# GpSimd in place of ScalarE issues one load of a multiply-and-GELU kernel

## The chip, the cores and the metric

The kernel runs on one core of a Trainium2 chip. A core has TensorE, VectorE, ScalarE, GpSimd and SyncE, which run their own instruction streams and meet through semaphores, and 16 DMA engines that move data between the device memory and the on-chip memory. In the profile the engines are called PE, DVE, ACT, POOL and SP; a name with a q behind it (SPq, POOLq) is the engine's instruction queue, where DMA issues, drains and semaphore operations are listed.

The metric is the device time of one execution in microseconds, taken as the median of several runs. The trace comes from one profiled execution, and its span runs from the first to the last instruction of the program; a little time lies around it.

## The reference

Two matrices of 1024 x 4096 in float32 are multiplied element by element, and the tanh form of GELU is taken of the product:

```python
z = x * y
return (0.5 * z * (1 + np.tanh(np.sqrt(2 / np.pi) * (z + 0.044715 * z ** 3)))).astype(np.float32)
```

Each matrix has 16.78 MB. Two are read and one is written, 50.33 MB in all.

## The kernel before

Each matrix is taken as one flat array and cut into three pieces (PIECES, line 14). A piece is laid over the 128 partitions of the on-chip memory, so that each partition gets one contiguous row of it: piece 0 has rows of 1,280 numbers (5 KB, 0.66 MB in all), piece 1 rows of 16,384 (64 KB, 8.39 MB) and piece 2 rows of 15,104 (59 KB, 7.73 MB). All of x lies on the chip at once in `xs`; y goes through a smaller buffer `ys`, whose places are used a second time (Y_LOADS, line 16, gives the place of each y piece; Y_FREE, line 18, the number of products that must be done before a place may be loaded again).

Each load or store of a piece is one DMA instruction with a semaphore of its own, which reaches 16 when all has landed. The loads and stores go out in this order:

- SyncE issues the load of x's piece 0 as its first instruction, and ScalarE that of x's piece 1 as its own first instruction. The function `_hoist` (lines 25 to 37) takes a DMA instruction out of the body and puts it into the program's first block, ahead of the drains and barriers that the launch code places there.
- SyncE then waits for x's piece 0 (line 81), and issues y's piece 1 and x's piece 2 one behind the other (lines 82 and 83).
- SyncE waits until three products are done and issues y's piece 2 into the place that they leave free; after the fourth product it issues y's piece 0 (lines 84 to 87).
- When y's piece 2 has landed and the results of piece 1 are done, SyncE stores piece 1, then piece 2, then piece 0 (lines 112 to 116). Lines 117 to 122 wait for the stores and clear the semaphores.

VectorE multiplies `xs` by `ys` in place, in 13 steps (STEPS, line 20): four of 4,096 columns over piece 1, seven of 2,048 and one of 768 over piece 2, one of 1,280 over piece 0. ScalarE follows step by step with the GELU, in place again (lines 99 to 110).

Around the body stands code of the launch. Line 137, the making of the program object, gives GpSimd four fills of constants and gives all engines a drain and a barrier: GpSimd drains its own queue, collects a semaphore from the other engines, and releases them. Line 59 (`tc.compile()`) adds two more such barriers. The body of every engine, SyncE's wait at line 81 included, comes behind these three; the two hoisted loads come ahead of them. In the program's first block GpSimd's order is one bookkeeping instruction (INC_SWDGE_SEM), the four fills, the drain, the barrier.

Of the kernel before, what the change touches and what calls it, by code (L numbers as in the profile page):

```python
# [1 line left out]

# [4 lines left out]


F32 = mybir.dt.float32
GELU = mybir.ActivationFunctionType.Gelu_apprx_tanh  # L10

PIECES = [(0, 1280), (1280, 17664), (17664, 32768)]

Y_LOADS = [(1280, 17664, 4056), (17664, 32768, 0), (0, 1280, 15104)]

Y_FREE = [0, 3, 4]

STEPS = [[4096] * 4, [2048] * 7 + [768], [1280]]  # L20
STORES = [(1280, 17664), (17664, 32768), (0, 1280)]
Y_BUF = 20440


def _hoist(nc, issued):

    here = nc.cur_bb.bb.instructions
    first = nc.main_func.blocks[0].instructions
    for ins in issued:
        del here[next(k for k, i in enumerate(here) if i is ins or i.name == ins.name)]  # L30
    engine = issued[0].engine
    at = next(
        k
        for k, i in enumerate(first)
        if i.engine == engine and type(i).__name__ == "InstDrain"
    )
    first[at:at] = issued


@with_exitstack  # L40
def kernel(
    ctx: ExitStack,
    tc: tile.TileContext,
    x: bass.AP,
    y: bass.AP,
    out: bass.AP,
):
    nc = tc.nc
    P = nc.NUM_PARTITIONS

    def columns(t, a, b):

        flat = t.flatten_outer_dims().rearrange("r c -> (r c)")
        pa, pb = next(q for q in PIECES if q[0] <= a and b <= q[1])
        return flat[P * pa : P * pb].rearrange("(p c) -> p c", p=P)[:, a - pa : b - pa]


    tc.close()
    tc.compile()

    xs = nc.alloc_sbuf_tensor("xs", [P, PIECES[-1][1]], F32).ap()
    ys = nc.alloc_sbuf_tensor("ys", [P, Y_BUF], F32).ap()
    sem_x = [nc.alloc_semaphore(f"sem_x{i}") for i in range(len(PIECES))]
    sem_y = [nc.alloc_semaphore(f"sem_y{i}") for i in range(len(Y_LOADS))]
    sem_mul = nc.alloc_semaphore("sem_mul")
    sem_act = nc.alloc_semaphore("sem_act")
    sem_o = [nc.alloc_semaphore(f"sem_o{i}") for i in range(len(STORES))]

    def load_x(i, engine=nc.sync):
        a, b = PIECES[i]  # L70
        return engine.dma_start(out=xs[:, a:b], in_=columns(x, a, b)).then_inc(sem_x[i], 16)

    def load_y(i):
        a, b, r = Y_LOADS[i]
        return nc.sync.dma_start(
            out=ys[:, r : r + b - a], in_=columns(y, a, b)
        ).then_inc(sem_y[i], 16)

    _hoist(nc, [load_x(0).ins])
    _hoist(nc, [load_x(1, nc.scalar).ins])  # L80
    nc.sync.wait_ge(sem_x[0], 16)
    load_y(0)
    load_x(2)
    for i in range(1, len(Y_LOADS)):
        if Y_FREE[i]:
            nc.sync.wait_ge(sem_mul, Y_FREE[i])
        load_y(i)

    nc.scalar.wait_ge(sem_x[0], 16)
    n = 0  # L90
    done = {}
    for i, (a, b, r) in enumerate(Y_LOADS):
        for j, (xa, xb) in enumerate(PIECES):
            if xa <= a < xb:
                nc.vector.wait_ge(sem_x[j], 16)
        nc.vector.wait_ge(sem_y[i], 16)  # L96
        c = a
        for w in STEPS[i]:
            nc.vector.tensor_mul(  # L99
                out=xs[:, c : c + w],  # L100
                in0=xs[:, c : c + w],
                in1=ys[:, r + c - a : r + c - a + w],
            ).then_inc(sem_mul, 1)
            n += 1
            done[c + w] = n
            nc.scalar.wait_ge(sem_mul, n)
            nc.scalar.activation(  # L107
                out=xs[:, c : c + w], in_=xs[:, c : c + w], func=GELU
            ).then_inc(sem_act, 1)
            c += w  # L110

    for i, (a, b) in enumerate(STORES):
        if i == 0:
            nc.sync.wait_ge(sem_y[-2], 16)
        nc.sync.wait_ge(sem_act, done[b])
        nc.sync.dma_start(out=columns(out, a, b), in_=xs[:, a:b]).then_inc(sem_o[i], 16)
    for i in range(len(STORES) - 1):
        nc.sync.wait_ge(sem_o[i], 16)
    nums = sorted(s.num for s in [*sem_x, *sem_y, *sem_o[:-1], sem_mul, sem_act])
    assert nums == list(range(nums[0], nums[-1] + 1))  # L120
    nc.sync.sem_clear(range(nums[0], nums[-1] + 1))
    nc.sync.wait_ge(sem_o[-1], 16).then_inc(sem_o[-1], -16)


# [1 line left out]
_INS = ['x', 'y']  # L126
_OUTS = [((1024, 4096), 'float32')]


# [23 lines left out]
```

## Time and profile before

| | |
|---|---|
| median of 3 runs | 119.83 us (119.7 to 119.85) |
| span of the profiled execution | 118.5 us, so 1.3 us lie around it |
| VectorE busy | 35.2 us, 13 instructions |
| ScalarE busy | 30.9 us, 14 instructions, one of them a table load of 1.28 us |
| GpSimd busy | 0.2 us, 4 instructions |
| bytes moved | 50.33 MB, 425 GB/s over the span |

Issue to landing of each load, from the list of DMA issues: x's piece 0 in 13.6 us (issued at 0.00), x's piece 1 in 30.4 us (issued by ScalarE at 0.12), y's piece 1 in 29.0 us (issued at 13.57), x's piece 2 in 46.5 us (issued at 13.96), y's piece 2 in 22.5 us (issued at 55.79). The three stores land 20.4 to 20.9 us after their issue.

How to read it: a page has the busy time of each engine, the span in 40 equal slices with the busy share in tenths and the rate of the DMA engines, the chain of work that ended last, and the groups of instructions with what ended the idle time before them. Queue instructions (drains, semaphores, DMA issues) are not counted as busy; they are found by asking for a line of the program. Of such a group the answer gives the count, the shortest, median and longest duration in ns, and the start of the first and last in us.

### The profile page before, as it was taken

How to read it: one execution, taken by the hardware profiler on the slowest of the kernel's cores; microseconds unless marked ns; L12 is line 12 of the kernel's file. 1: busy time of each engine (PE TensorE's matmuls, PEld its weight loads, DVE VectorE, ACT ScalarE, POOL GpSimd, SP SyncE). 2: the span in 40 equal slices, each digit the busy share in tenths (PEclk: the TensorE clock that was granted, in tenths of full speed). 3: DMA queues.
4: the chain of work that ended last, by engine and by line, in shares of the span. 5: the costliest groups of instructions: out<-in, count | busy, mean ns of one | idle time of the engine just before them, and what ended most of it. 6: DMA issues, size and time to landing. Idle time of an engine off the chain costs nothing.

```text
span 118.5 us, 83 instructions
## 1 busy us (share of the span) xinstructions
DVE 35.2 (30%) x13; ACT 30.9 (26%) x14; POOL 0.2 (0%) x4
## 2 busy tenths in 40 slices
DVE  0000000000000069999920000059999940000000
ACT  0000000000000000999975000006998990000000
POOL 0000000000000000000000000000000000000000
DMA  9888899889988897798797797798899887977975
GB/s 492 382 382 382 354 597 464 354 354 465 597 354 354 354 632 347 326 632 347 326 632 347 326 632 347 326 575 354 354 531 531 354 354 326 653 326 326 653 326 221
DMA packets 1296, 50.33 MB, mean 425 GB/s; under 512 B 144, under 2 KB 144, under 8 KB 528
## 3 DMA queue, kind: packets, MB, share of 16 engines
q1 hardware_dynamic: 1152, 41.94, 82.3%
q10 hardware_dynamic: 144, 8.39, 16.5%
HBM read 33.55 MB, written 16.78 MB: 425 GB/s over the span
## 4 chain that ended last, share of the span: by engine, by line
DMA 55%; DVE 24%; ACT 3%; issue 1%; DVEq 0%
DMA ys<-in_y_dram 43%; DVE xs L99 24%; DMA xs<-in_x_dram 11%; ACT xs L107 3%; DVEq L96 0%
## 5 line engine op out<-in xcount | busy, mean ns | idle before, releaser
L99 DVE TENSOR_TENSOR xs<-xs,ys 128x2048 f32<-128x2048 f32 (+3 forms) x13 | 35.2, 2778 | 60.9 <-DMA ys<-in_y_dram 60.9
L107 ACT ACTIVATE xs<-xs 128x2048 f32<-128x2048 f32 (+3 forms) x13 | 29.6, 2300 | 19.6 <-DVE xs L99 19.6
L107 ACT ACT_TABLE_LOAD x1 | 1.3, 1283 | 47.2 <-DVE xs L99 47.2
L137 POOL MEMSET const-uint8-127<- 128x1 uint8 x1 | 0.1, 102 | 0.0
L137 POOL MEMSET const-bfloat16-1.0<- 128x1 bf16 x1 | 0.1, 101 | 0.0
L137 POOL MEMSET const-float32-0.0<- 128x1 f32 x1 | 0.1, 98 | 0.2 <-issue 0.2
L137 POOL MEMSET const-float32-1.0<- 128x1 f32 x1 | 0.1, 98 | 0.0
## 6 DMA issues: line engine op xcount, KB each, us to landing
xs<-in_x_dram SPq DMA_DIRECT2D x1, 7552.0 KB, 46.5
ys<-in_y_dram SPq DMA_DIRECT2D x1, 7552.0 KB, 22.5
out_dram<-xs SPq DMA_DIRECT2D x1, 7552.0 KB, 20.4
xs<-in_x_dram SPq DMA_DIRECT2D x1, 640.0 KB, 13.6
ys<-in_y_dram SPq DMA_DIRECT2D x1, 640.0 KB, 19.7
out_dram<-xs SPq DMA_DIRECT2D x1, 640.0 KB, 20.8
xs<-in_x_dram ACTq DMA_DIRECT2D x1, 30.4
ys<-in_y_dram SPq DMA_DIRECT2D x1, 29.0
```

The lines of the kernel that those rows point to most:

```text
L99: nc.vector.tensor_mul(out=xs[:, c : c + w], in0=xs[:, c : c + w], in1=ys[:, r + c - a : r + c - a + w],).then_inc(sem_mul, 1)
L107: nc.scalar.activation(out=xs[:, c : c + w], in_=xs[:, c : c + w], func=GELU).then_inc(sem_act, 1)
L137: nc = _bacc.Bacc("TRN2", target_bir_lowering=False, num_devices=1)
```

## The change

The load of x's piece 1 is issued by GpSimd instead of ScalarE. The hoisting function now looks for the engine's first drain or fill, whichever comes first: on GpSimd that is the first constant fill, so that the DMA stands behind INC_SWDGE_SEM and ahead of the four fills, the drain and the barriers. SyncE and ScalarE have no fills in that block, so nothing moves for the load of x's piece 0. The bytes, rows, places and semaphores stay as they are.

```diff
@@ -32,7 +32,7 @@
     at = next(
         k
         for k, i in enumerate(first)
-        if i.engine == engine and type(i).__name__ == "InstDrain"
+        if i.engine == engine and type(i).__name__ in ("InstDrain", "InstMemset")
     )
     first[at:at] = issued
 
@@ -77,7 +77,7 @@
     _hoist(nc, [load_x(0).ins])
-    _hoist(nc, [load_x(1, nc.scalar).ins])
+    _hoist(nc, [load_x(1, nc.gpsimd).ins])
     nc.sync.wait_ge(sem_x[0], 16)
     load_y(0)
     load_x(2)
```

## The prediction

> **What bounds the kernel now.** I read the slices first, then windows, the chain, the first microseconds instruction by instruction, and what SyncE's queue waits for. In slices and windows the DMA engines are full from the second microsecond to the last:
>
> ```profile
> DMA  9888899889988897798797797798899887977975
> GB/s 492 382 382 382 354 597 464 354 354 465 597 354 354 354 632 347 326 632 347 326 632 347 326 632 347 326 575 354 354 531 531 354 354 326 653 326 326 653 326 221
> ```
> ```profile
> 0.00:1.00 1.00, 0.00 (x0) 0.00 (x0) 0.20 (x4) 1.00 0.00 0
> 1.00:42.60 41.60, 0.00 (x0) 0.00 (x0) 0.00 (x0) 1.00 1.03 442
> ```
>
> The last two columns of a window are DMA share and GB/s. Nothing moves for 1.0 us, SyncE's first load starts, and then 442 GB/s go by until y's 64 KB rows (y0) have landed; 50.33 MB over the span are 425. A transfer is booked where it starts, so a share can read a little over 1. By the trace's records of single transfers the first starts at 1.01 and the last ends at 118.1, with 116.3 us of packets on each engine between: at most 0.8 us is idle. So bytes are the bound, and a change costs what it adds of empty DMA time, whichever engine computes.
>
> Which transfers must be kept supplied is in the chain (start, length, what) and in SyncE's waits:
>
> ```profile
> 0.00 13.56 DMA xs<-in_x_dram
> 13.56 0.02 issue
> 13.57 28.99 DMA ys<-in_y_dram
> 42.56 0.03 issue
> ```
> ```profile
> SPq L75 <- DVE xs L99: 45.4, 2, 41.4
> ...
> SPq L75 <- DMA xs<-in_x_dram: 12.1, 1, 12.1
> ```
>
> SyncE loads x's small piece (0.66 MB, called x0 here), waits for it (12.1 us), issues y0 at 13.57 and x's last piece (x2) at 13.96. Only ScalarE's load of x's 64 KB rows (x1, 8.39 MB) bridges the engines from about 2.3 to 17.4 us, the first transfer of y0. x0 lands so late because its rows alternate on each engine with x1's, 2.42 us a row: x0's first five rows are through when x1 starts at 2.2 to 2.6 us, and the other three and the completion mark each wait behind one row of x1. x1 is through near 27.7. There are 14 us between the issue of y0 and the end of x1, and that slack is what keeps the engines full.
>
> The beginning, by instruction and then by line:
>
> ```profile
> 0.12 0.36 ACTq L71 DMA_DIRECT2D xs<-in_x_dram  x1
> 0.23 0.10 POOL L137 MEMSET const-float32-0.0<- 128x1 f32 x1 [0.23 <-issue]
> ...
> 0.33 0.10 POOL L137 MEMSET const-uint8-127<- 128x1 uint8 x1
> ```
> ```profile
> L137 POOLq INC_SWDGE_SEM  x1: 27/27/27, 0.1 to 0.1; - x1
> ...
> L137 POOLq DRAIN  x1: 181/181/181, 0.3 to 0.3; - x1
> ...
> L137 ACTq DRAIN  x1: 145/145/145, 0.5 to 0.5; - x1
> L137 SPq EVENT_SEMAPHORE  x1: 17/17/17, 0.8 to 0.8; - x1
> ```
> ```profile
> L59 POOLq DRAIN  x2: 34/38/41, 0.9 to 1.2; - x2
> ...
> L59 SPq EVENT_SEMAPHORE  x2: 17/17/17, 1.1 to 1.5; - x2
> ```
>
> Line 137 ends with a barrier of all engines, and line 59 holds two more. GpSimd is the hub: it drains, collects the others, releases them. SyncE is out of the third barrier at 1.5, and only then can it reach its wait for x0 and the issue of y0. So y0 stands behind three drains of GpSimd's queue.
>
> **The change, part by part.** *Removed:* one issue on ScalarE, 0.36 us at 0.12. ScalarE's next work is a table load at 47.17 that waits for VectorE: worth nothing. Its drain (0.5) may come 0.36 earlier, but SyncE idles 12.1 us behind the barrier: nothing.
>
> *Added:* the same issue on GpSimd, at about 0.16, behind the 27 ns instruction and ahead of fills, DRAIN and barriers. Two prices are not in the trace.
>
> First, when x1's first row starts. Rows near it: SyncE's issue at 0.00 moves at 1.01, so 1.0 after issue; ScalarE's, at 0.12 behind SyncE's, moves at 2.2, so 2.1 after. By these GpSimd's rows start at 1.2 to 2.3. x0 alone, eight rows per engine at a mean of 0.24 us, fills the engines until 1.01 + 1.9 = 2.9. I take 2.3, within that cover, so zero; each microsecond after 2.9 costs one until y0 fills the hole. The ends are 0 and, for a start two microseconds worse than the worst row, 1.4. The Trainium skill ("DMA: Bandwidth & Descriptors", Latency and other measured facts) gives a first byte about 0.6 us after an issue from sync or scalar and about 1 us from GpSimd; our row of 1.0 is already longer than that 0.6, so the page's difference of 0.4 on that row would give an estimated start near 1.6, also under cover.
>
> Second, what stands behind the issue on GpSimd's queue: four fills (about 0.2 us), the DRAIN, the three barriers, and through them SyncE's y0 and x2 and all compute. The DRAIN's rows bound its price from both sides. ScalarE's DRAIN took 145 ns while 8.39 MB of ScalarE's own load were in flight until 30 us: a drain need not wait for a transfer. That is the low end, 0. But GpSimd's DRAIN, starting at 0.3 for 181 ns, ended at 0.48, about 0.05 after the last fill (0.33 + 0.10): it does wait for what GpSimd issued. And GpSimd alone has an instruction in this preamble that keeps count of DMA semaphores (INC_SWDGE_SEM): its DMA issues are work that the engine's own queue tracks, where ScalarE's are handed off. I take it that the DRAIN holds until x1 has landed; that is the high end, worked out now.
>
> x0 and x1 are 9.04 MB, at 425 GB/s 21.3 us from 1.01: the engines would turn to the next transfer at 22.3. For y0, 17.43 MB had gone by at its landing, 41.0 us from 1.01 or 42.0, and it was seen at 42.56; so a landing is seen some 0.5 us after the mean engine is through: x1 at 22.8. The DRAIN ends 0.05 later. From its end to SyncE's last release is now 0.48 to 1.49, 1.0 us: 23.85. SyncE's wait for x0 is long over, it issues y0 at once, and the first byte follows 1.0 us later: 24.85. The engines stand empty for 24.85 - 22.3 = 2.55 us. Off that comes about 0.2: where x1 and y0 now alternate, 12 to 27 us, an engine's records show gaps of 0.02 to 0.1 at the changes of queue, and one queue at a time mostly shows none. Net 2.35 us.
>
> Downstream all shifts alike. In both orders y0 is through when x0, x1 and y0 have gone by, x2 follows, y's second load is released by VectorE's third product (55.79) with x2 running to 60; compute, loads and stores keep their distances. No cover is lost there and none is gained.
>
> The sum: the profiled execution has a span of 118.5, and the median of the runs is 119.83, 1.3 us more, which lies around the span. 118.5 + 2.35 = 120.85 of span, 122.2 with what lies around it. Bounds for this case: a quicker way (landing seen 0.4 late, barriers at their spacing of 0.33 each, first byte after 0.85 as with the first store) adds 1.7, thus 121.5; a start of x1 a microsecond past its cover and slower barriers add 3.8, thus 123.6.
>
> **The rivals.** *The DRAIN lets go, and nothing changes.* For: ScalarE's 145 ns. Against: the 181 ns and the counting instruction above. Then a start of x1 anywhere between 1.5 and 2.9 only moves x0's landing between some 3 and 20 us; y0 is issued before x1 is through (22 at the earliest), and the engines never run dry: 119.8. The Trainium skill says as much of a change of issuer ("DMA: Bandwidth & Descriptors", Issuing engines are not separate DMA queues): the transfers run on the same 16 engines and interleave whoever starts them, so only issue time is saved. The trace bears that out for two queues from 2.3 to 27.7 us, and for the barrier no row decides.
>
> *The DRAIN lets go, but GpSimd's rows come late.* From 2.9 until x1 starts the engines are empty. x0 then lands near 3.2, y0 is issued at 3.6 and moves by 4.6, so the hole is 1.7 at most: 120.2 to 121.5. For: no row shows a GpSimd issue, and it is the engine's first work. Against: 2.1 us is the worst row. If GpSimd also cut the rows smaller, x1 would fall behind y0 and land late; no row speaks for it.
>
> *The DRAIN lets go, and GpSimd's rows come too early.* If x1 starts before 1.5, x0's rows alternate with all eight of x1, and x0 lands only when x1 is through: the hole is landing, issue and first byte, 0.4 + 1.0 + 0.2 of spread: 121.4. For: SyncE's 1.0 us. Against: GpSimd would have to be as quick as that.
>
> *Faster.* One mechanism: with the alternation gone, or x1's first row sooner, some of the 0.8 us of idle DMA time between first and last transfer goes. It decides only if the DRAIN lets go and over 0.24 is won: 119.2 to 119.5. Against: the first byte at 1.01 is SyncE's and untouched, and most of the gaps lie behind 27 us.
>
> **How the numbers follow.** DRAIN holds: 0.70, 122.2, its own range 121.5 to 123.6. No change: 0.17. Late: 0.07. Too early: 0.03. Faster: 0.03. A measurement of this kernel tells 0.2% (0.24 us) from no change; so slower 0.70 + 0.07 + 0.03 = 0.80, same 0.17, faster 0.03. The case's own range holds some 0.63, and with late and too early about 0.72; to leave out no more than 0.2 it must reach the unchanged time: 119.6 to 123.6.
>
> **What would show it.** In the profile after: GpSimd's DRAIN of line 137 lasting some 22 us, SyncE's releases at lines 137 and 59 near 23 to 24 us, y0 issued near 24 with a landing 18 to 19 us later, x1 landing 22 to 23 us after its issue, a DMA-free stretch of over 2 us before 25 us, and VectorE starting near 45 instead of 42.66. Wrong it would be if that DRAIN stays under a microsecond; then x0's landing and the issue of y0 tell which rival it is. If the DRAIN holds and the loss is small, then a landing is seen sooner, or the barriers pass quicker, than their rows say.

## The result, and the profile after

The changed kernel takes 124.61 us (median of 4 runs, 124.13 to 124.8), the kernel before 119.8 us beside it. The ratio is 1.0398, with a 95% interval of 1.0383 to 1.0413: slower by 4.8 us. The forecast was 122.2 us, in a range of 119.6 to 123.6: the measured time lies 1.0 us above its upper end. The sign was right, its mechanism was right, and its size was half of the true one. A run more than 1.5% above the fastest of its kernel counts as slow and stands in no ratio: below, one of six in the changed kernel's second series, and three of four, the profiled one among them, with a quarter of x1 on GpSimd.

The profiled execution of the changed kernel has a span of 123.7 us and a time of 124.53. The first instructions, then parts of lines 137 and 59 (count, shortest/median/longest in ns, start of the first and last in us); three dots stand for lines left out:

```profile
0.00 0.38 SPq L71 DMA_DIRECT2D xs<-in_x_dram  x1
0.72 0.65 POOL L71 DMA_DIRECT2D xs<-in_x_dram  x1 [0.72 <-issue]
1.37 0.12 POOL L137 MEMSET const-float32-0.0<- 128x1 f32 x1
...
25.91 0.33 SPq L75 DMA_DIRECT2D ys<-in_y_dram  x1
```
```profile
L137 POOLq EVENT_SEMAPHORE  x2: 17/17/17, 25.1 to 25.1; - x2
...
L137 ACTq DRAIN  x1: 8/8/8, 0.1 to 0.1; - x1
...
L137 PEldq DRAIN  x1: 8/8/8, 0.3 to 0.3; - x1
L137 SPq DRAIN  x1: 131/131/131, 0.4 to 0.4; - x1
L137 POOLq DRAIN  x1: 24212/24212/24212, 0.8 to 0.8; - x1
...
L137 SPq EVENT_SEMAPHORE  x1: 17/17/17, 25.2 to 25.2; - x1
```
```profile
L59 SPq EVENT_SEMAPHORE  x2: 17/17/17, 25.5 to 25.8; - x2
```

GpSimd's drain took 0.18 us before; now it takes 24.2 us, from 0.80 to 25.01. Every other engine has drained by 0.6 us. The list of issues gives the landing of GpSimd's load (last number, us after its issue at 0.72, so at 24.9):

```profile
xs<-in_x_dram POOLq DMA_DIRECT2D x1, 24.2
```

GpSimd releases them at 25.1, two more barriers pass, and SyncE issues y's 64 KB rows (y0) at 25.91, where it was 13.57. SyncE's waits and the chain say the same:

```profile
SPq L137 <- PEq L137: 24.7, 1, 24.7
```
```profile
25.85 0.06 issue
25.91 21.83 DMA ys<-in_y_dram
```

The profile puts this wait down to PE's queue, but PE had drained at 0.3: the wait is the barrier, and the only drain of it that ends near 25 us is GpSimd's.

Windows, with the last two columns DMA share and GB/s, first of the changed kernel, then of the kernel before:

```profile
1.00:23.20 22.20, 0.00 (x0) 0.00 (x0) 0.59 (x5) 1.00 0.99 407
23.20:26.60 3.40, 0.00 (x0) 0.00 (x0) 0.00 (x0) 1.00 0.00 0
26.60:47.70 21.10, 0.00 (x0) 0.00 (x0) 0.00 (x0) 1.00 1.05 443
```
```profile
23.20:26.60 3.40, 0.00 (x0) 0.00 (x0) 0.00 (x0) 1.00 0.71 308
```

In 3.4 us no transfer starts at all. From y0's landing on (47.74, before 42.56) the chain runs 5.2 us later, and its distances behind it have not changed.

The records of single transfers give the sum for a mean DMA engine (starts and ends are means over the 16 engines). The whole shift of 5.2 us of span is made before y0 has landed:

| Part | Before | After | Adds |
|---|---|---|---|
| x0's last row ends, x1's first starts | no hole | 2.99, 3.30 | 0.3 |
| rows of x1, mean of 8 per engine | 2.44 us | 2.51 us | 0.55 |
| rows of y0, mean of 8 per engine | 2.42 us | 2.50 us | 0.65 |
| rows of x0, mean of 8 per engine | 0.24 us | 0.23 us | -0.1 |
| x1's last row ends, y0's first starts | no hole | 23.36, 27.06 | 3.7 |

x0 is x's small piece and x1 its 64 KB rows, as in the prediction. The hole of 3.7 us has four pieces: 1.24 from the mean end of x1 to its last row on any engine (24.60), 0.41 until the drain ends (25.01), 0.90 through three barriers to SyncE's issue (25.91), and 1.15 to the mean first row of y0 (27.06).

### The profile page after: what moved, and what is told of

It is laid out like the page before. It is cut to its first block, busy times and chain, and to the rows that moved or that the text cites. A ratio compares the mean times of both kernels' runs of the same rounds, so it can differ in the third digit from the quotient of the medians.

```text
span 123.7 us, 83 instructions
## 1 busy us (share of the span) xinstructions
DVE 35.2 (28%) x13; ACT 30.9 (25%) x14; POOL 0.9 (1%) x5
## 4 chain that ended last, share of the span: by engine, by line
DMA 36%; DVE 23%; ACT 3%; issue 1%; DVEq 0%
DMA ys<-in_y_dram 36%; DVE xs L99 23%; ACT xs L107 3%; DVEq L96 0%
## 5 line engine op out<-in xcount | busy, mean ns | idle before, releaser
L71 POOL DMA_DIRECT2D xs<-in_x_dram x1 | 0.7, 652 | 0.7 <-issue 0.7
## 6 DMA issues: line engine op xcount, KB each, us to landing
ys<-in_y_dram SPq DMA_DIRECT2D x1, 7552.0 KB, 22.5
xs<-in_x_dram POOLq DMA_DIRECT2D x1, 24.2
```

## The experiments

Each run names the theory that the drain of GpSimd holds SyncE's issue of y0, and a rival.

**GpSimd issues x1 behind the barriers.** The hoisting is undone, the issuer stays GpSimd.

```diff
-    _hoist(nc, [load_x(1, nc.gpsimd).ins])
+    load_x(1, nc.gpsimd)
```

> GpSimd still issues x's 64 KB rows (x1), but in the body, behind the three barriers, so that no drain stands behind the issue. Theory (the loss is the wait of GpSimd's drain for x1, which holds SyncE's issue of y's 64 KB rows (y0) behind the barriers): the drain of line 137 is back under 0.5 us, y0 is issued near 3.6, and what is left is GpSimd's late first row. In the changed kernel that row starts 2.1 to 3.5 us after the issue at 0.73; from an issue near 1.55 that is 3.7 to 5.1, while x0 is through at 3.0: a hole of about 1.2 us less what y0 fills from 4.6 on, and slower first rows: 120.8 to 121.6 us. Rival (a load issued by GpSimd is itself slow, wherever it stands): near 124 us, with x1's rows still slower than 2.5 us in the mean.

Measured: 120.84 us (120.74 to 120.97), ratio 1.0087 (1.0072 to 1.0102). The drain and the issues of this kernel:

```profile
L137 POOLq DRAIN  x1: 186/186/186, 0.3 to 0.3; - x1
```
```profile
1.93 0.65 POOL L71 DMA_DIRECT2D xs<-in_x_dram  x1 [1.49 <-POOLq L59]
3.66 0.33 SPq L75 DMA_DIRECT2D ys<-in_y_dram  x1
```

With no drain behind it, the same load by the same engine costs 1.0 us, not 4.8. x1's first rows start at 3.29 to 3.93, 0.4 us after x0 is through in the mean, and take 3.10 us instead of 2.58. So about a fifth of the loss stays without the hold, and the place ahead of the drain brings the rest. The fifth is no exact share: the issue comes 1.2 us later here (1.93 instead of 0.72).

**ScalarE issues x1, and SyncE waits for it.** The kernel before, with the drain's hold put where it acts:

```diff
     nc.sync.wait_ge(sem_x[0], 16)
+    nc.sync.wait_ge(sem_x[1], 16)
     load_y(0)
```

> The kernel before, with ScalarE issuing x1, and one wait added: SyncE waits for x1 to have landed before it issues y0. This puts the drain's wait where it acts without GpSimd. Theory: x1 is through at 22.4 in the mean and landed at 22.8, seen at 23.1, y0 is issued at 23.2 and its first rows start at 24.2 to 24.4, a hole of 1.9 us; if first rows after a hole are slow on any queue (3.07 against 2.42 us for y0 in the changed kernel), another 0.6: 122.0 to 122.4 us, about half of the loss of 4.8; the other half would then be GpSimd's part (three barriers 0.9, late and staggered start, spread at the end). Rival (holding y0 is harmless, the loss is in GpSimd's queue): 119.8 to 120.2 us.

Measured: 122.38 us (122.23 to 122.53), ratio 1.0216 (1.02 to 1.0231). SyncE's wait for x1, and the issue that follows it:

```profile
SPq L82 <- DMA xs<-in_x_dram: 21.8, 1, 21.8
```
```profile
23.34 0.33 SPq L75 DMA_DIRECT2D ys<-in_y_dram  x1
```

Here GpSimd issues nothing, and half of the loss is there. x1 ends at 22.54 in the mean, y0's first rows start at 24.51: a hole of 1.97. y0's rows then take 2.50 in the mean and the first ones 3.07, another 0.65. Together that is the 2.6 by which this span (121.1) exceeds 118.5. What GpSimd adds to reach 123.7 is again 2.6: x1 through 0.8 later (23.36 instead of 22.54), its last row 0.9 further behind the mean (1.24 instead of 0.38), and 0.9 more from the last row to the issue of y0 (1.31 instead of 0.42), for the way leads through the drain and three barriers.

**The drain stays, and y0 is issued ahead of it.**

```diff
-    nc.sync.wait_ge(sem_x[0], 16)
-    load_y(0)
-    load_x(2)
+    _hoist(nc, [load_y(0).ins])
+    _hoist(nc, [load_x(2).ins])
```

> The changed kernel, with SyncE's issues of y0 and of x's last piece (x2) taken ahead of its drain too, and its wait for x0 taken away. GpSimd's drain still waits for x1, but nothing that the DMA engines need stands behind it. Theory: the drain lasts about 40 us, because x1 now alternates with y0, VectorE is released before y0 lands near 42.5, the engines never run dry, and the time is that of the kernel before: 119.5 to 120.3 us. Rival (the GpSimd-issued load is slow in itself, or the held barriers cost in another way): above 121.5 us.

Measured: 120.1 us (119.97 to 120.68), ratio 1.0028 (1.0016 to 1.0039). GpSimd's drain, and the same windows as above:

```profile
L136 POOLq DRAIN  x1: 41994/41994/41994, 0.8 to 0.8; - x1
```
```profile
1.00:23.20 22.20, 0.00 (x0) 0.00 (x0) 0.60 (x5) 1.00 1.07 455
23.20:26.60 3.40, 0.00 (x0) 0.00 (x0) 0.00 (x0) 1.00 0.71 308
```

The drain holds all engines for 42.0 us, longer than in the changed kernel, because x1 now alternates with y0; the hole is gone, the windows from 1.0 to 26.6 us are those of the kernel before, and 4.5 of the 4.8 us are back. What the hold costs is, for the most part, the transfers that stand behind it.

The rest is 0.25 us of time, but 0.8 of span (median 119.3 of seven runs, 118.4 to 118.6 before); the section on where the time is counted from shows why the two part. In the profiled run, the longest of the seven, it is 1.4 us of span. There VectorE starts 1.15 us later than before (43.81 instead of 42.66), since the drain and the barriers come between the landing and it, and y's second load is issued as much later. Yet no hole comes of that: the first rows of this load start at 59.70 in the mean, before at 59.68. But three of them take 3.2 to 3.6 us instead of 2.23, and the load lands 1.33 us later. Whether the later issue has to do with that was not tried.

**The load behind the fills, twice, and the changed kernel again.** The place relative to the four constant fills is undone:

```diff
-        if i.engine == engine and type(i).__name__ in ("InstDrain", "InstMemset")
+        if i.engine == engine and type(i).__name__ == "InstDrain"
```

> The changed kernel with the load placed behind the four constant fills and still ahead of GpSimd's drain: the place relative to the fills undone. Theory: the fills take 0.2 us, so the load starts at most 0.2 us later and the drain waits for it as before: 124.4 to 124.9 us, as the changed kernel (124.6). Rival (the place as first instruction matters, by a first-use cost of GpSimd ahead of its fills): 0.5 us or more away from 124.6.

Measured: 124.05 us (123.72 to 124.72), a little under what was expected. Both places then ran once more, side by side.

> The changed kernel once more, beside the next run, on the same chip. The engines' last rows of x1 ended between 22.7 and 24.6 us in its first profile, and the latest was the engine whose first row had started last (4.24). Theory (that spread is a part of the loss that differs from execution to execution): 124.1 to 124.8 us again.

> The load behind the four fills, as before, beside the run above. It gave 124.05 against the changed kernel's 124.61, with x1's first rows starting within 0.7 us of each other instead of 1.4. If the place matters for how evenly the engines start, the difference of about 0.5 us comes back, and the spread of the first rows with it; if it was the scatter of the runs, the two are within 0.2 us.

Measured: the changed kernel 124.08 us (123.24 to 125.19, 6 runs), the load behind the fills 124.67 us (124.02 to 125.61, 6 runs). The order has turned round, so these runs do not show that the place relative to the fills matters. They scatter by 1.6 to 2 us, and in the four profiles that goes with how evenly x1's first rows start and its last ones end: 0.67, 0.84, 1.43 and 1.82 us between the first and the last engine's start, last ends at 23.48, 23.61, 24.60 and 25.25 us, and spans of 122.4, 122.7, 123.7 and 124.3. In the changed kernel's first profile the engine that starts last (4.24) also ends last (24.60); in its second it does not (3.72, and 23.05 where the last end is 23.61). The drain waits for the last end.

**A quarter of x1 on GpSimd.**

```diff
-    _hoist(nc, [load_x(1, nc.gpsimd).ins])
+    a, b = PIECES[1]
+    _hoist(nc, [nc.gpsimd.dma_start(
+        out=xs[:32, a:b], in_=columns(x, a, b)[:32]).then_inc(sem_q, 16).ins])
+    _hoist(nc, [nc.scalar.dma_start(
+        out=xs[32:, a:b], in_=columns(x, a, b)[32:]).then_inc(sem_x[1], 16).ins])
```

Not shown are the new semaphore, here and in the next two edits, and VectorE's wait for the second part, here and in the next one.

> GpSimd issues only 32 of the 128 rows of x1 ahead of its drain (two per DMA engine), ScalarE the other 96. Theory (the drain holds until GpSimd's own transfer has landed, and this costs only if the engines run dry before y0 is issued): GpSimd's part alternates with the others and lands near 15 us, the drain of line 137 lasts about 14 us, y0 is issued near 18, x1's other rows run until 22: no hole, 119.7 to 120.4 us. Rival (any load issued by GpSimd ahead of the drain costs, by its own slow start or by the held barriers): 121 us or more.

Measured: 143.2 us (139.9 to 143.83), for a reason that neither theory had: the rows of 65,536 bytes took 5.48 us (GpSimd's) and 4.91 us (ScalarE's) in the mean instead of 2.42. So it says nothing on the slack. One thing can be read from it, in its list of issues (last number: us to landing) and its drain:

```profile
xs<-in_x_dram ACTq DMA_DIRECT2D x1, 48.9
xs<-in_x_dram POOLq DMA_DIRECT2D x1, 35.9
```
```profile
L143 POOLq DRAIN  x1: 35932/35932/35932, 0.8 to 0.8; - x1
```

The drain ended at 36.7, behind GpSimd's own part (issued at 0.7, landed at 36.6) and 12 us ahead of ScalarE's: it waits for its own engine's transfer, and not for all that move.

The same split, both parts on ScalarE, the 96 partitions first and the 32 behind them:

```diff
-    _hoist(nc, [load_x(1, nc.scalar).ins])
+    a, b = PIECES[1]
+    _hoist(nc, [nc.scalar.dma_start(
+        out=xs[32:, a:b], in_=columns(x, a, b)[32:]).then_inc(sem_x[1], 16).ins])
+    _hoist(nc, [nc.scalar.dma_start(
+        out=xs[:32, a:b], in_=columns(x, a, b)[:32]).then_inc(sem_q, 16).ins])
```

> The split of x1 into 96 and 32 partitions again, both parts issued by ScalarE, none by GpSimd. In the run with a quarter on GpSimd the rows took 4.9 to 5.5 us instead of 2.42. If the split over partitions makes the rows slow, they are as slow here and x1 lasts some 38 us instead of 19: 136 to 142 us. If it was GpSimd's part in it, the rows take 2.4 us and the time is 119.8.

Measured: 142.99 us, ratio 1.193, with rows of 4.75 us in the mean and no load of GpSimd's in it. So it is the split that doubles a row's time, and not GpSimd. Whether it is the smaller number of partitions or the second load, and why, was not tried.

**A small load ahead of GpSimd's drain.** The test of the slack again, with rows left alone. x1 is on ScalarE; the extra 1 KB lands where nothing is needed yet. The function `_hoist` looks for fills too, as in the changed kernel.

```diff
     _hoist(nc, [load_x(1, nc.scalar).ins])
+    _hoist(nc, [nc.gpsimd.dma_start(
+        out=ys[:16, :16], in_=columns(x, 0, 1280)[:16, :16]).then_inc(sem_q, 16).ins])
     nc.sync.wait_ge(sem_x[0], 16)
     load_y(0)
     load_x(2)
+    nc.sync.wait_ge(sem_q, 16)
```

> The kernel before, x1 on ScalarE, and one small extra load added: GpSimd loads 1 KB (16 partitions of 64 bytes, one row per DMA engine) into a place of y's buffer that is free until y's last 60 KB rows come, as its first instruction ahead of its fills. Theory (GpSimd's drain holds until GpSimd's own transfer has landed, and that costs only when the engines run dry before y0 is issued): the small row and its mark each wait for one or two rows of x1, so it lands at 7 to 11 us, the drain of line 137 lasts 7 to 11 us, x0 lands at 13 as before, y0 is issued near 13.6: 119.7 to 120.1 us. Rival (a load of GpSimd ahead of the barriers costs by itself): 120.8 us or more.

Measured: 119.34 us (119.23 to 119.43), ratio 0.9955 (0.9941 to 0.9968). The drain, the small load's landing, and the issues:

```profile
L141 POOLq DRAIN  x1: 9886/9886/9886, 0.8 to 0.8; - x1
```
```profile
ys<-in_x_dram POOLq DMA_DIRECT2D x1, 1.0 KB, 9.9
```
```profile
0.73 0.61 POOL L82 DMA_DIRECT2D ys<-in_x_dram  x1 [0.73 <-issue]
1.34 0.12 POOL L141 MEMSET const-float32-0.0<- 128x1 f32 x1
...
16.10 0.33 SPq L76 DMA_DIRECT2D ys<-in_y_dram  x1
```

A drain of 9.9 us costs nothing: x0 lands near 16 with three queues taking turns, y0 is issued at 16.10, and x1's last rows run until 22.5 to 25.4. This is the slack of the prediction, seen from its safe side. But the kernel was half a microsecond faster than forecast, with a span of 118.6, where the kernel before has 118.5. Time minus span had dropped from 1.33 to 0.83.

**Where the time is counted from.** To the kernel above, one fill by VectorE is added ahead of VectorE's drain.

```diff
+    _hoist(nc, [nc.vector.memset(ys[:, 20:21], 0.0).ins])
```

> The kernel with the small extra load on GpSimd, and one fill of a single column added that VectorE does ahead of its drain. That kernel had the span of the kernel before (118.6 and 118.5) and yet 0.5 us less time: 0.83 us lie around its span instead of 1.33. In the runs so far time minus span is 1.3 wherever GpSimd's first counted instruction starts near 0.24, and 0.83 wherever it starts near 0.73. Theory (the time is counted from the first instruction that the profile counts as busy, on whichever engine): VectorE's fill starts near 0.12 to 0.2, so 1.35 to 1.45 lie around the span again and the time is 119.9 to 120.1 us. Rival (with the load first, GpSimd's own way into or out of the program is shorter): 119.2 to 119.5 us, as without the fill.

Measured: 119.91 us (119.81 to 120.06), ratio 1.0005 (0.9996 to 1.0014). A useless fill made the kernel 0.57 us slower, with the same span (118.5):

```profile
0.00 0.39 SPq L72 DMA_DIRECT2D xs<-in_x_dram  x1
...
0.15 0.06 DVE L82 MEMSET ys<- 128x1 f32 x1
0.73 0.61 POOL L83 DMA_DIRECT2D ys<-in_x_dram  x1 [0.73 <-issue]
```

In all of these the time is the span, less the start of the first instruction that counts as busy, plus 1.56: 118.52 - 0.23 + 1.56 for the kernel before, 123.69 - 0.72 + 1.56 for the changed one, 118.60 - 0.73 + 1.56 with the small load, 118.50 - 0.15 + 1.56 here; the 1.56 is fitted to these runs. So the 119.34 is a later start of the count, and the work ends no sooner.

This bears on three comparisons above. Wherever GpSimd's load is its first counted instruction (0.72), the time is 0.5 us short against the kernel before (0.23): the loss of the changed kernel is 4.8 us of time and 5.2 of span, that of y0 ahead of the drain 0.25 and 0.8. And with the load behind the fills the first fill starts at 0.24, so 0.5 of the 0.6 us between the two series that ran side by side is the count.

**All issues ahead of the drain, ScalarE kept.** The edit made for y0 above, on the kernel before.

```diff
-    nc.sync.wait_ge(sem_x[0], 16)
-    load_y(0)
-    load_x(2)
+    _hoist(nc, [load_y(0).ins])
+    _hoist(nc, [load_x(2).ins])
```

> The kernel before with y0 and x2 issued by SyncE ahead of its drain too, without its wait for x0; x1 stays on ScalarE. Theory (the kernel before is bound by its transfers, which follow one another with 0.8 us of idle time at most): 119.5 to 120.0 us, so no gain worth the name. If taking the wait away lets the engines start or hand over better, under 119.5.

Measured: 119.82 us (119.68 to 120.0), ratio 0.9998 (0.9989 to 1.0007). SyncE's wait for x0 costs nothing and gains nothing; no run shows a version whose work ends clearly sooner than that of the kernel before (118.5 us of span in the median, as there).

## Why the prediction was right in kind and wrong in size

The cost of the hold is the step that failed: 2.35 us of span were forecast, 5.2 measured. Two terms of the sum make up most of it. From the mean end of x1 to the end of the drain the sum had 0.55 us (landing and drain), and 1.65 were measured. For the transfers' rows the sum had no change, and slow first rows added 1.1. The range did not reach far enough because its upper bound, 3.8, was made of a late start of x1 and slower barriers, which came to 0.3 and to nothing.

- *What bounds the kernel.* Right. Every run that left a hole between transfers was slower, and the one that filled it again, with the drain still held, came back to 120.1. The idle time was read too high: the records sum to 117.0 us of packets for a mean engine, as the page's 82.3% and 16.5% of the span do, and not to 116.3, so by that count 0.1 us of the 117.1 is idle, where the prediction allowed 0.8.
- *The DRAIN holds until x1 has landed.* Right, and this was the open question: 24.2 us against the "some 22" forecast. It ends 0.08 us after the landing (0.05 was forecast), and 0.41 after the last completion mark. ScalarE's drain with a load in flight took 0.15 us in the kernel before and in the run with the small load, so the two engines' drains differ. Whether the counting instruction, from which the prediction argued, has to do with that is not shown.
- *When x1's first row starts.* Mis-sized. The step took an issue at 0.16 and a start at 2.3, under x0's cover until 2.9. The issue came at 0.72, and the rows started from 2.81 to 4.24, 3.30 in the mean, where x0 was through at 2.99: a hole of 0.3. The distance from issue to first row, 2.1 to 3.5 us and 2.6 in the mean, is longer than both rows that bounded it (1.0 and 2.1). It is longer, too, than what the Trainium skill states for GpSimd ("DMA: Bandwidth & Descriptors", Latency and other measured facts: a first byte after about 1 us); here the measurement decides.
- *A landing is seen 0.5 us after the mean engine is through.* Mis-sized, and the largest single miss: 1.65 (1.24 of spread over the engines, 0.41 to the drain's end). The 0.5 came from y0's landing, whose rows SyncE's queue starts evenly: 0.66 us between the first and the last of its first rows in the kernel before. Even there it was 0.7, since y0's rows end at 41.85 in the mean and not at 42.0. GpSimd's rows started over 1.4 us.
- *Barriers 1.0, first byte 1.0.* Right: 0.90 and 0.95 to the first row, 1.15 to the mean. (The lower bound of 1.7 comes out of its parts with two barriers at 0.33; with all three they give 2.0.)
- *y0 lands 18 to 19 us after its issue.* This sign does not fit the prediction's own sum, which has the issue near 24 and VectorE's start near 45, 21 us apart. Measured: 21.83, the slow first row included.
- *What the prediction left out:* the first row after a hole is slow. y0's first rows took 3.07 us after the hole and x1's 3.04, against 2.42 and 2.58. Over both loads, less 0.1 on x0, that is 1.1 us, nearly half of the whole forecast. It is no property of GpSimd: SyncE's y0 showed it in the run with ScalarE (3.07), and GpSimd's x1 did not where y0 kept the engines busy (2.43).
- *The credit of 0.2 for gaps at changes of queue.* Not seen: the parts of the table sum to 5.1 of 5.2 without it. In the kernel before x1 and y0 alternate from 17.4 us on, not from 12.
- *The time around the span stays 1.3.* Wrong: 0.83, which hides 0.5 us of the loss.

In sum: forecast 2.55 - 0.2 of span, measured 5.2; of the 2.8 between them 1.1 are the landing, 1.1 the slow first rows, 0.3 the late start, 0.2 the credit, and 0.1 the first row of y0. Beside the rival in which nothing changes stood the rule that transfers from all issuers share the same engines and interleave (the Trainium skill, "DMA: Bandwidth & Descriptors", Issuing engines are not separate DMA queues). On the transfers the run with y0 ahead of the drain agrees with it: x1 from GpSimd and y0 from SyncE interleave, and the time is 0.28% above that of before, the span 0.7%. What decided was the instruction behind the issue.

## What to carry to other kernels

Before a load is moved to another engine's queue, read what stands behind it there: GpSimd's drain waits for its own transfers, and through a barrier that wait reached every engine here. Price a hole in the transfers from the mean engine's last row to the mean engine's first one, with the spread up to the last engine's end in it, and add a slow first row at its end; the spread and the restart here were as large as the latencies between them. A hold costs only from the point where the transfer engines run dry, so count what is already issued ahead of it.

## What the runs showed of the hardware

- GpSimd's drain waits until the transfers that GpSimd issued have landed (drains of 9.9, 24.2, 36 and 42 us; in all eight profiles with such a load the drain ended 0.08 us after the landing); ScalarE's and SyncE's drains took 0.15 us or less with transfers in flight.
- A load issued by GpSimd started its rows 1.4 us after the start of its issue at the earliest (1.93 to 3.29, behind the barriers) and 3.5 us at the latest in the changed kernel's first profile (0.72 to 4.24). From the first engine to the last it took 0.6 to 1.8 us where no other load took turns with it, and in the four profiles with the load ahead of the drain and y0 behind it the span grew with this spread, from 122.4 to 124.3 us.
- After a hole in the transfers, even one of 0.3 us, the first rows of 64 KB took 2.9 to 3.4 us in the mean instead of 2.42 to 2.6, on SyncE's and on GpSimd's queue. Why was not tried.
- x1 split into a load to 96 and one to 32 partitions took 4.75 to 5.5 us per 64 KB row in the mean, as one load to all 128 partitions 2.42.
- The time runs as if it were counted from the first instruction that the profile counts as busy (time minus span 1.3 us with that at 0.23, 0.8 at 0.72, 1.4 at 0.15); the DMA issues of SyncE and ScalarE ahead of it do not start it.
